# Recurrent layer of a two-layer encoder: scans, gelus and products behind the last convolution, the square root in another form, and the split of two weight slabs on another engine

## The chip, the core and the metric

The kernel runs on one core of a Trainium2 chip. TensorE (PE) multiplies matrices, VectorE (DVE), ScalarE (ACT) and GpSimd (POOL) work elementwise, and SyncE (SP) issues most of the DMA transfers. Each engine works through its own queue of instructions in order and waits on semaphores for the others. The metric is the device time of one execution in microseconds; the median of three runs is 1107.1 us (1106.69 to 1107.58).

## The reference

The input is a sequence of 512 tokens of width 1024. Two layers each add a mixer and a squared-relu MLP to it, with an RMS norm ahead of each. The mixer of the first layer is a stick-breaking attention, that of the second the gated recurrent block which the change is about:

```python
proj = h @ w_in
gate = jax.nn.gelu(proj[..., :RG_WIDTH])
xc = causal_depthwise_conv(proj[..., RG_WIDTH:], conv_w, conv_b)
xh = xc.reshape(B, S, RG_BLOCKS, RG_BLOCK_DIM)
r = jax.nn.sigmoid(jnp.einsum('bshi,hij->bshj', xh, w_a).reshape(B, S, RG_WIDTH) + b_a)
i = jax.nn.sigmoid(jnp.einsum('bshi,hij->bshj', xh, w_x).reshape(B, S, RG_WIDTH) + b_x)
log_a = (-RG_C * r.astype(jnp.float32)) * jax.nn.softplus(-lam.astype(jnp.float32))
a = jnp.exp(log_a)
mult = jnp.sqrt(-jnp.expm1(2.0 * log_a))
bterm = mult * (i * xc).astype(jnp.float32)
_, hs = lax.associative_scan(lru_combine, (a, bterm), axis=1)
y = hs.astype(h.dtype) * gate
return y @ w_o
```

All matrices are float32, and the recurrence runs along the 512 tokens: each state is a times the state before it plus bterm.

## The kernel before

Activations lie transposed: 128 of the 1024 features on the partitions, 512 tokens along the free axis, so a layer's activation is eight chunks (C = 8) of 128 x 512. To keep float32 accuracy with fast matmuls, each operand is split into a rounded part and the rest (`wh`, `wl` for weights, `xgh`, `xgl` or `bh`, `bl` for activations), and a product takes three matmuls (`three`, lines 187 to 191). A weight slab of 128 x 1024 is loaded by SP, rounded on ACT (line 178) and then gets its rest in one of two ways: DVE subtracts (line 184), or, while `adding[0]` is set, POOL negates the rounded part (line 181) and a DMA that adds brings the raw slab to it (line 182). Six buffers for the parts run ahead of the matmuls.

Ahead of the layer, `residual` (line 626) adds each chunk of the MLP's output to the stream (`add_x`, line 624), splits it (`halves`: `xgh` on ACT at line 117, `xgl` on DVE at line 118), squares it on ACT (line 138) and lets POOL sum the squares into `ssq` (line 139). A matmul with ones (line 143) sums over the partitions, and `inv_rms` turns that into `r` (lines 123 and 124).

The recurrent layer runs over chunks by a list written out by hand (line 978 on). Its steps are:

- `conv(c)`: a slab product of 24 matmuls in `dense_in`, times `r` (line 906), the convolution as one scaled copy on ACT (line 914, `begin`) and three taps on DVE (line 916, the last is `tap`), then the split of the result on ACT (line 922) and DVE (line 923), and the gate weights. These steps are issued with high priority.
- `gates(c)`: six matmuls (lines 933 to 935) that read this split, two sigmoids on ACT (lines 938 and 939), and a product on DVE (line 940).
- `recur(chunks)`: for three chunks at a time, tanh and exp on ACT (lines 949 and 951), products on DVE and POOL (lines 952 to 954), then the square root on ACT (line 957), a product (line 958) and the scan on DVE (line 959).
- `gate(c)`: a slab product of 24 matmuls and a product with `r` (line 965).
- `gated(chunks)`: gelu on ACT (line 971), the product with the scan's result on DVE (line 973), and the split into `bh` and `bl` (lines 974 and 975), which the product with w_ro reads.

Sigmoid and tanh, exp, square root and gelu need different activation tables, and each change of table is a load on ACT. `after(x)` holds an instruction back until x has been issued on its engine; beyond that, the order on ACT, DVE, POOL and SP is set when the program is built, by a scheduler that simulates the engines. The order on PE within the layer is the order of the program.

The steps at the end of the list are conv 7, the recurrence of chunks 3 to 5, gates 6, gate 5, gated 0 to 5, gate 6, gates 7, the recurrence of chunks 6 and 7, gate 7, gated 6 and 7. Behind it four columns of w_ro (lines 990 to 997) are multiplied chunk by chunk. The buffer tags that matter are `a0` and `tanh` with two buffers each, `aa` with five, `bt` with six (it holds `xc`), `om` with eight, `z` with six.

Of the kernel before, what the change touches and what calls it, by code (L numbers as in the profile page):

```python
# [11 lines left out]
F32 = mybir.dt.float32  # L12
F32R = mybir.dt.float32r
AF = mybir.ActivationFunctionType
ALU = mybir.AluOpType
PSUM = bass.MemoryType.PSUM

P = 128
S = 512
# [28 lines left out]
def hybrid_encoder(  # L48
# [24 lines left out]
    V, A, G, PE = nc.vector, nc.scalar, nc.gpsimd, nc.tensor  # L73
# [15 lines left out]
    def f(ap):  # L89
        return ap.bitcast(F32)  # L90
# [4 lines left out]
    def col(name):  # L95
        o, n = COLS[name]
        return colt[:, o : o + n]
# [68 lines left out]
    adding = [False]  # L166
# [46 lines left out]
    with ExitStack() as actx:  # L213
# [252 lines left out]
        turns = [0]  # L466
# [366 lines left out]
    with ExitStack() as rctx:  # L833
        rp1 = rctx.enter_context(tc.tile_pool(name="rp1", bufs=1))
        rp2 = rctx.enter_context(tc.tile_pool(name="rp2", bufs=2))
        rctx.enter_context(tc.manual_schedule(engines={mybir.EngineType.PE}))


        lam = col("lam")

        def small(name):
            return rp1.tile([P, C], F32, tag=name, name=name)

        ab, pp, den, s1, s2, pl, c8, c4 = (
            small(n) for n in ("ab", "pp", "den", "s1", "s2", "pl", "c8", "c4")
        )
        V.tensor_scalar(ab, lam, -1.0, None, ALU.mult)
        V.tensor_tensor(ab, ab, lam, ALU.max)
        A.activation(pp, ab, AF.Sigmoid, scale=-1.0)
        V.tensor_scalar(den, pp, -1.0, 2.0, ALU.mult, ALU.add)  # L850
        V.reciprocal(den, den)
        V.tensor_tensor(s1, pp, den, ALU.mult)
        V.tensor_tensor(s2, s1, s1, ALU.mult)
        V.tensor_scalar(pl, s2, 1.0 / 17, 1.0 / 15, ALU.mult, ALU.add)
        for n in (13, 11, 9, 7, 5, 3, 1):
            V.tensor_tensor(pl, pl, s2, ALU.mult)
            V.tensor_scalar(pl, pl, 1.0 / n, None, ALU.add)
        V.tensor_tensor(pl, pl, s1, ALU.mult)
        V.tensor_scalar(den, lam, -1.0, 0.0, ALU.mult, ALU.max)
        V.scalar_tensor_tensor(c8, pl, 2.0, den, ALU.mult, ALU.add)  # L860
        V.tensor_scalar(c4, c8, RG_C * 0.5, None, ALU.mult)
        V.tensor_scalar(c8, c8, -RG_C, None, ALU.mult)


        graws = []
        for i in range(2):
            t = rp1.tile([P, 2, P], F32, tag=f"graw{i}", name=f"graw{i}")
            G.memset(t, 0.0)
            graws.append(t)

        def gate_weights(c):
            raw = graws[c % 2]
            for j in range(2):
                a = slice(j * HD, (j + 1) * HD)
                nc.sync.dma_start(out=raw[a, :, a], in_=w_gate[a, c])
            wh = rp2.tile([P, 2, P], F32R, tag="gh", name="gh", bufs=3)
            wl = rp2.tile([P, 2, P], F32R, tag="gl", name="gl", bufs=3)
            A.copy(wh, raw)
            V.tensor_tensor(wl, raw, f(wh), ALU.subtract)
            return wh, wl  # L880

        cw = col("conv")
        r = None
        mark = None

        def after(act):

            return tc.issue_after(act.ins) if act is not None else nullcontext()

        xc, aa, om, z, hs, gin = {}, {}, {}, {}, {}, {}  # L890
        turns = [0, 0]

        def dense_in(i):

            nonlocal r
            adding[0] = turns[0] >= 4
            ps = dense(w_in[i], xgh, xgl, tag=("acc", "t")[turns[0] % 2])
            turns[0] += 1
            if r is None:
                r = sq.inv_rms()  # L900
            return ps

        def conv(c):

            ps = dense_in(C + c)
            V.tensor_tensor(ps, ps, r, ALU.mult)
            aa[c], xc[c], om[c] = (
                rp1.tile([P, S], F32, tag=t, name=t, bufs=n)
                for t, n in (("aa", 5), ("bt", 6), ("om", C))
            )  # L910
            x0 = xc[c]
            nonlocal begin, tap
            taps = [cw[:, i * C + c : i * C + c + 1] for i in range(4)]
            begin = A.activation(x0, ps, AF.Identity, bias=col("conv_b")[:, c : c + 1], scale=taps[3])
            for d in range(1, 4):
                tap = V.scalar_tensor_tensor(
                    x0[:, d:], ps[:, : S - d], taps[3 - d], x0[:, d:], ALU.mult, ALU.add
                )

            i = C - 3 + c % 3  # L920
            xch, xcl = bh[:, i, :], bl[:, i, :]
            A.copy(xch, x0)
            V.tensor_tensor(xcl, x0, f(xch), ALU.subtract)
            gin[c] = (xch, xcl, *gate_weights(c))

        def gates(c):
            nonlocal sig
            xch, xcl, gh, gl = gin[c]
            pg = []
            for i in range(2):  # L930
                pi = bank("oozz"[turns[1] % 4])
                turns[1] += 1
                PE.matmul(pi, gh[:, i, :], xch, start=True, stop=False)
                PE.matmul(pi, gl[:, i, :], xch, start=False, stop=False)
                PE.matmul(pi, gh[:, i, :], xcl, start=False, stop=True)
                pg.append(pi)
            with after(mark):
                A.activation(aa[c], pg[0], AF.Sigmoid, bias=col("b_a")[:, c : c + 1])
                sig = A.activation(om[c], pg[1], AF.Sigmoid, bias=col("b_x")[:, c : c + 1])
            V.tensor_tensor(xc[c], om[c], xc[c], ALU.mult)  # L940

        def recur(chunks):
            nonlocal mark

            for c in chunks:
                a0 = rp2.tile([P, S], F32, tag="a0", name="a0")
                th = rp2.tile([P, S], F32, tag="tanh", name="tanh")
                with after(sig):
                    ex = A.activation(th, aa[c], AF.Tanh, scale=c4[:, c : c + 1])
                with after(ex):  # L950
                    ex = A.activation(a0, aa[c], AF.Exp, scale=c8[:, c : c + 1])
                V.scalar_tensor_tensor(a0, a0, 1.0, th, ALU.add, ALU.mult)
                G.tensor_scalar(aa[c], a0, -1.0, 1.0, ALU.mult, ALU.add)
                V.scalar_tensor_tensor(om[c], a0, 2.0, a0, ALU.subtract, ALU.mult)
            for c in chunks:
                with after(ex):
                    mark = A.activation(om[c], om[c], AF.Sqrt, scale=-1.0)
                V.tensor_tensor(xc[c], xc[c], om[c], ALU.mult)
                V.tensor_tensor_scan(om[c], aa[c], xc[c], 0.0, ALU.mult, ALU.add)
                hs[c] = om[c]  # L960

        def gate(c):
            ps = dense_in(c)
            z[c] = rp1.tile([P, S], F32, tag="z", name="z", bufs=6)
            V.tensor_tensor(z[c], ps, r, ALU.mult)

        def gated(chunks):
            for c in chunks:

                with after(mark), after(begin):  # L970
                    A.activation(z[c], z[c], AF.Gelu_apprx_tanh)
                with after(tap):
                    V.tensor_tensor(z[c], hs[c], z[c], ALU.mult)
                A.copy(bh[:, c, :], z[c])
                V.tensor_tensor(bl[:, c, :], z[c], f(bh[:, c, :]), ALU.subtract)

        sig = begin = tap = None
        for what, c in (
            (conv, 0), (conv, 1), (conv, 2), (gate, 0), (gates, 0), (gates, 1), (conv, 3), (gates, 2),
            (gate, 1), (conv, 4), (gates, 3), (recur, range(3)), (gate, 2), (conv, 5), (gates, 4),  # L980
            (gate, 3), (conv, 6), (gates, 5), (gate, 4), (conv, 7), (recur, range(3, 6)), (gates, 6),
            (gate, 5), (gated, range(6)), (gate, 6), (gates, 7), (recur, range(6, C)), (gate, 7),
            (gated, range(6, C)),
        ):
            with tc.high_priority() if what is conv else nullcontext():
                what(c)

        adding[0] = False

        begun = {}  # L990
        for c in range(4):
            wh, wl = slab(w_ro[c])
            begun[c] = bank("oozz"[c]), wh, wl
        for k in range(C):
            for c in range(4):
                ps, wh, wl = begun[c]
                three(ps, bh[:, k, :], bl[:, k, :], wh[:, k, :], wl[:, k, :], k == 0, k == C - 1)
# [149 lines left out]
```

## Time and profile before

The profiled execution took 1106.54 us. TensorE is the engine with the most work; a table by stage from the view of windows:

| Stretch (us) | length | PE busy | DVE busy | ACT busy | POOL busy | granted PE clock |
|---|---|---|---|---|---|---|
| 500 to 590 | 90 | 90.00 | 63.29 | 39.11 | 20.92 | 1.00 |
| 590 to 610 | 20 | 18.93 | 6.27 | 6.89 | 8.97 | 1.00 |
| 610 to 630 | 20 | 17.76 | 12.49 | 8.84 | 13.27 | 0.91 |
| 630 to 670 | 40 | 40.00 | 24.10 | 25.94 | 24.10 | 1.00 |
| 670 to 690 | 20 | 20.00 | 17.14 | 15.49 | 9.27 | 1.00 |
| 690 to 710 | 20 | 16.91 | 19.96 | 18.40 | 0.00 | 0.92 |
| 710 to 750 | 40 | 40.00 | 28.03 | 20.23 | 7.85 | 1.00 |
| 750 to 850 | 100 | 100.00 | 65.33 | 49.56 | 5.44 | 1.00 |
| whole span | 1104.80 | 1079.34 | 769.53 | 564.49 | 221.25 | 0.993 |

The recurrent layer lies between about 598 and 732 us. A stretch in which PE's busy time falls short of the length is one in which it waited, and the granted clock below 1.00 says that the array ran at reduced speed for a part of it. A row of a timeline gives the start, the duration, the engine, the line, the operation with the tile that it writes and those that it reads, and in brackets the idle time before it with what ended that.

### The profile page before, as it was taken

How to read it: one execution, taken by the hardware profiler on the slowest of the kernel's cores; microseconds unless marked ns; L12 is line 12 of the kernel's file. 1: busy time of each engine (PE TensorE's matmuls, PEld its weight loads, DVE VectorE, ACT ScalarE, POOL GpSimd, SP SyncE). 2: the span in 40 equal slices, each digit the busy share in tenths (PEclk: the TensorE clock that was granted, in tenths of full speed). 3: DMA queues.
4: the chain of work that ended last, by engine and by line, in shares of the span. 5: the costliest groups of instructions: out<-in, count | busy, mean ns of one | idle time of the engine just before them, and what ended most of it. 6: DMA issues, size and time to landing. Idle time of an engine off the chain costs nothing.

```text
span 1104.8 us, 13615 instructions
## 1 busy us (share of the span) xinstructions
PE 1079.3 (98%) x5052; PEld 893.6 (81%) x5052; DVE 769.5 (70%) x984; ACT 564.5 (51%) x831; POOL 221.2 (20%) x232
## 2 busy tenths in 40 slices
PE   9999999998999999999999899899999999999997
PEld 7888888786888888888888688788888888888886
DVE  7878787729694597599465558956695597599522
ACT  6766676726446444344344467844446344343422
POOL 2444444523000000001223655022000000002220
PEclk9999999999999999999999999999999999999999
DMA  7735453426205305302333775242305305303502
GB/s 236 201 100 138 129 140 94 156 71 228 96 1 189 116 1 190 115 1 77 114 109 114 165 166 153 76 154 94 96 20 174 112 20 174 112 1 93 174 1 77
DMA packets 43458, 123.62 MB, mean 112 GB/s; under 512 B 7680, under 2 KB 8448, under 8 KB 43392
## 3 DMA queue, kind: packets, MB, share of 16 engines
q1 hardware_dynamic: 41088, 115.94, 33.3%
q0 software_dynamic: 1728, 6.29, 3.0%
q8 instruction: 40, 0.66, 0.2%
q10 hardware_dynamic: 576, 0.52, 0.1%
q14 instruction: 26, 0.21, 0.1%
HBM read 101.76 MB, written 2.10 MB: 94 GB/s over the span
## 4 chain that ended last, share of the span: by engine, by line
PE 90%; DVE 4%; ACT 3%; DMA 1%; issue 1%; POOL 0%; SPq 0%; DVEq 0%; ACTq 0%; POOLq 0%
PE ps_acc L190 7%; PE ps_acc L189 7%; PE ps_acc L191 7%; PE ps_o L191 4%; PE ps_o L189 4%; PE ps_o L190 4%; PE ps_t L190 4%; PE ps_t L189 4%; PE ps_t L191 4%; PE ps_z L189 3%; PE ps_z L190 3%; PE ps_z L191 3%; PE ps_t L758 2%; PE ps_t L757 2%; PE ps_t L759 2%; PE ps_acc L758 2%
## 5 line engine op out<-in xcount | busy, mean ns | idle before, releaser
L178 ACT CAST wh<-raw 128x1024 fp32r<-128x1024 f32 (+2 forms) x144 | 128.6, 911 | 159.1 <-PE ps_o L191 47.2
L184 DVE TENSOR_TENSOR wl<-raw,wh 128x1024 fp32r<-128x1024 f32 (+2 forms) x132 | 143.9, 1103 | 30.1 <-ACT wh L178 30.0
L690 POOL TENSOR_TENSOR bl<-u,bh 128x512 fp32r<-128x512 f32 x16 | 31.4, 1962 | 556.5 <-ACT bh L689 540.8
L189 PE MATMUL ps_acc<-xgh,wh 128*128 128x512 f32 x320 | 128.2, 401 | 1.3 <-ACT xgh L117 1.1
L732 ACT CAST wh<-b 128x1024 fp32r<-128x1024 f32 x72 | 75.7, 1051 | 102.5 <-PE ps_acc L759 16.2
L191 PE MATMUL ps_acc<-xgl,wh 128*128 128x512 f32 x320 | 126.0, 394 | 0.3 <-DVE xgl L118 0.3
L190 PE MATMUL ps_acc<-xgh,wl 128*128 128x512 f32 x320 | 126.1, 394 | 0.0
L733 DVE TENSOR_TENSOR wl<-b,wh 128x1024 fp32r<-128x1024 f32 x72 | 88.0, 1222 | 27.0 <-ACT wh L732 27.0
L493 DVE TENSOR_TENSOR_SCAN scan<-keep,later 128x128 f32<-128x128 f32 (+1 forms) x64 | 56.8, 888 | 22.3 <-ACT keep L485 15.9
L191 PEld LDWEIGHTS ps_acc<-xgl,wh 128*128 128x128 f32 x320 | 60.5, 189 | 13.9 <-DVE xgl L118 0.8
L189 PEld LDWEIGHTS ps_acc<-xgh,wh 128*128 128x128 f32 x320 | 60.6, 189 | 12.6 <-ACT xgh L117 1.5
L190 PEld LDWEIGHTS ps_acc<-xgh,wl 128*128 128x128 f32 x320 | 60.6, 189 | 10.8 <-DVE wl L160 0.5
L685 ACT ACTIVATE u<-u 128x512 f32<-128x512 f32 x64 | 39.6, 630 | 54.4 <-DVE u L684 54.3
L189 PE MATMUL ps_t<-xgh,wh 128*128 128x512 f32 x168 | 67.0, 399 | 0.0
L190 PE MATMUL ps_t<-xgh,wl 128*128 128x512 f32 x168 | 66.6, 397 | 0.0
L191 PE MATMUL ps_t<-xgl,wh 128*128 128x512 f32 x168 | 66.3, 395 | 0.0
L191 PE MATMUL ps_o<-xgl,wh 128*128 128x512 f32 x152 | 60.4, 397 | 3.9 <-DVE xgl L118 3.9
L497 POOL TENSOR_TENSOR w<-w,scan 128x128 f32<-128x128 f32 (+1 forms) x64 | 52.5, 822 | 56.9 <-DVE scan L493 55.6
L189 PE MATMUL ps_o<-xgh,wh 128*128 128x512 f32 x152 | 61.3, 403 | 0.0
L190 PE MATMUL ps_o<-xgh,wl 128*128 128x512 f32 x152 | 59.8, 394 | 0.0
L189 PE MATMUL ps_z<-xgh,wh 128*128 128x512 f32 x128 | 50.0, 391 | 0.0
L190 PE MATMUL ps_z<-xgh,wl 128*128 128x512 f32 x128 | 49.9, 389 | 0.0
(339 smaller groups left out, 2791.1 us busy)
## 6 DMA issues: line engine op xcount, KB each, us to landing
raw<-in_w_m SPq DMA_DIRECT2D x72, 512.0 KB, 3.5
b<-in_w_dn SPq DMA_DIRECT2D x36, 512.0 KB, 4.3
raw<-in_w_in SPq DMA_DIRECT2D x16, 512.0 KB, 3.5
raw<-in_w_qk SPq DMA_DIRECT2D x12, 512.0 KB, 3.8
raw<-in_w_dn SPq DMA_DIRECT2D x12, 512.0 KB, 3.5
wl<-raw POOLq DMA_DIRECT2D x12, 512.0 KB, 5.1
x<-in_xT SPq DMA_DIRECT2D x16, 256.0 KB, 3.9
raw<-in_w_ro SPq DMA_DIRECT2D x8, 512.0 KB, 3.4
```

The costliest lines, as they stand in the source:

```text
L178: A.copy(wh[:, k, :], raw[:, k, :])
L184: V.tensor_tensor(wl[:, k, :], raw[:, k, :], f(wh[:, k, :]), ALU.subtract)
L189: PE.matmul(ps, wh, ah, start=start, stop=False)
L190: PE.matmul(ps, wl, ah, start=False, stop=False)
L191: PE.matmul(ps, wh, al, start=False, stop=stop)
L493: V.tensor_tensor_scan(sc[:, S - n : S][:, ::-1], keep[:, :n][:, ::-1], later[:, S - n :][:, ::-1], 1.0, ALU.mult, ALU.max,)
L497: G.tensor_tensor(wt, wt, sc[:, S - n + 1 : S + 1], ALU.mult)
L685: A.activation(t, t, AF.Square)
L690: G.tensor_tensor(bl[:, c, :], t, f(bh[:, c, :]), ALU.subtract)
L732: A.copy(wh, raw)
L733: V.tensor_tensor(wl, raw, f(wh), ALU.subtract)
L758: PE.matmul(ps[i], h[:, piece, ts], wl[:, jj, :], start=False, stop=False)
```

## The change

The subtraction on DVE serves two more slabs of w_in: `adding` is set from the seventh slab on and no longer from the fifth. The conv's split gives its two instructions the names `high` and `low`. The sigmoids of `gates` are issued behind the last conv's scaled copy. In `recur`, with t = tanh, 1 - a^2 is written as t (1 + a)^2, so that the root is sqrt(t) (1 + a): tanh is written into `om`, `d` takes the place of the tile `tanh`, (1 + a) is multiplied into `xc`, and the root reads t. The scans of chunks 0 to 5 are issued behind the last tap, the gelus behind `high` and the products behind `low` of the last conv. Some lines move by one or two (952 to 958 keep their numbers; the scan is now 961, gate's product 967, gelu 972, the product 974, the split 975 and 976).

```diff
         def dense_in(i):
 
             nonlocal r
-            adding[0] = turns[0] >= 4
+            adding[0] = turns[0] >= 6
...
             xch, xcl = bh[:, i, :], bl[:, i, :]
-            A.copy(xch, x0)
-            V.tensor_tensor(xcl, x0, f(xch), ALU.subtract)
+            high = A.copy(xch, x0)
+            low = V.tensor_tensor(xcl, x0, f(xch), ALU.subtract)
...
-            with after(mark):
+            with after(mark), after(begin):
                 A.activation(aa[c], pg[0], AF.Sigmoid, bias=col("b_a")[:, c : c + 1])
                 sig = A.activation(om[c], pg[1], AF.Sigmoid, bias=col("b_x")[:, c : c + 1])
...
             for c in chunks:
                 a0 = rp2.tile([P, S], F32, tag="a0", name="a0")
-                th = rp2.tile([P, S], F32, tag="tanh", name="tanh")
+                d = rp2.tile([P, S], F32, tag="d", name="d")
                 with after(sig):
-                    ex = A.activation(th, aa[c], AF.Tanh, scale=c4[:, c : c + 1])
+                    ex = A.activation(om[c], aa[c], AF.Tanh, scale=c4[:, c : c + 1])
                 with after(ex):
                     ex = A.activation(a0, aa[c], AF.Exp, scale=c8[:, c : c + 1])
-                V.scalar_tensor_tensor(a0, a0, 1.0, th, ALU.add, ALU.mult)
-                G.tensor_scalar(aa[c], a0, -1.0, 1.0, ALU.mult, ALU.add)
-                V.scalar_tensor_tensor(om[c], a0, 2.0, a0, ALU.subtract, ALU.mult)
+                V.scalar_tensor_tensor(d, a0, 1.0, om[c], ALU.add, ALU.mult)
+                G.tensor_scalar(aa[c], d, -1.0, 1.0, ALU.mult, ALU.add)
+                V.scalar_tensor_tensor(xc[c], a0, 1.0, xc[c], ALU.add, ALU.mult)
             for c in chunks:
                 with after(ex):
-                    mark = A.activation(om[c], om[c], AF.Sqrt, scale=-1.0)
+                    mark = A.activation(om[c], om[c], AF.Sqrt)
                 V.tensor_tensor(xc[c], xc[c], om[c], ALU.mult)
-                V.tensor_tensor_scan(om[c], aa[c], xc[c], 0.0, ALU.mult, ALU.add)
+
+                with after(tap if c < 6 else None):
+                    V.tensor_tensor_scan(om[c], aa[c], xc[c], 0.0, ALU.mult, ALU.add)
                 hs[c] = om[c]
...
         def gated(chunks):
             for c in chunks:
-
-                with after(mark), after(begin):
+                with after(mark), after(high):
                     A.activation(z[c], z[c], AF.Gelu_apprx_tanh)
-                with after(tap):
+                with after(low):
                     V.tensor_tensor(z[c], hs[c], z[c], ALU.mult)
                 A.copy(bh[:, c, :], z[c])
                 V.tensor_tensor(bl[:, c, :], z[c], f(bh[:, c, :]), ALU.subtract)
```

More of the change, by code (lines that the diff above doesn't have):

```diff
@@ L911, in conv @@
             x0 = xc[c]
-            nonlocal begin, tap
+            nonlocal begin, tap, high, low
             taps = [cw[:, i * C + c : i * C + c + 1] for i in range(4)]
@@ L975, in gated @@
                 V.tensor_tensor(bl[:, c, :], z[c], f(bh[:, c, :]), ALU.subtract)
-        sig = begin = tap = None
+        sig = begin = tap = high = low = None
         for what, c in (
```

## The prediction

> **What bounds the kernel now.** I read the page first, then the list of what TensorE waited for, then the timelines of the stretch from 596 to 716 us, where the recurrent layer lies.
>
> ```profile
> span 1104.8 us, 13615 instructions
> PE 1079.3 (98%) x5052; PEld 893.6 (81%) x5052; DVE 769.5 (70%) x984; ACT 564.5 (51%) x831; POOL 221.2 (20%) x232
> PE 90%; DVE 4%; ACT 3%; DMA 1%; issue 1%; POOL 0%; SPq 0%; DVEq 0%; ACTq 0%; POOLq 0%
> ```
>
> TensorE sets the time: 98% busy, 90% of the chain that ended last. The order of its instructions is the same in both built programs, so the change can only take away or add TensorE waits. Between 600 and 760 us these are all of them:
>
> ```profile
> PE ps_z L935 <- DVE bl L923: 3.1, 1, 3.1
> PE ps_z L143 <- POOL ssq L139: 1.9, 1, 1.9
> PE ps_acc L189 <- ACT xgh L117: 1.1, 1, 1.1
> PE ps_acc L191 <- DVE xgl L118: 0.3, 1, 0.3
> ```
>
> Two places, then: the last three rows are the end of the norm before the layer, the first is the gates of chunk 7. A timeline shows what they cost (start, duration, the wait in brackets):
>
> ```profile
> 608.50 0.39 PE L191 MATMUL ps_acc<-xgl,wh 128*128 128x512 f32 x1
> 609.95 0.50 PE L189 MATMUL ps_acc<-xgh,wh 128*128 128x512 f32 x1 [1.06 <-ACT xgh L117]
> 611.01 0.50 PE L191 MATMUL ps_acc<-xgl,wh 128*128 128x512 f32 x1 [0.33 <-DVE xgl L118]
> 613.43 1.13 PE L143 MATMUL ps_z<-ssq,ones 128*128 128x512 f32 x2 [1.92 <-POOL ssq L139]
> ...
> 614.66 0.63 PE L190 MATMUL ps_t<-xgh,wl 128*128 128x512 f32 x1
> ...
> 618.03 0.40 PE L189 MATMUL ps_t<-xgh,wh 128*128 128x512 f32 x1
> ...
> 703.15 0.40 PE L934 MATMUL ps_z<-bh,gl 128*128 128x512 f32 x1
> 706.64 0.75 PE L935 MATMUL ps_z<-bl,gh 128*128 128x512 f32 x1 [3.09 <-DVE bl L923]
> ...
> 710.17 0.40 PE L190 MATMUL ps_t<-xgh,wl 128*128 128x512 f32 x1
> 710.40 0.39 PE L191 MATMUL ps_t<-xgl,wh 128*128 128x512 f32 x1
> ```
>
> At full speed one matmul follows the other after 710.40 - 710.17 = 0.23 us. The wait at L935 lasts from 703.38 (703.15 + 0.23) to 706.64: 3.26 us. Then the array runs slowly: 706.64 to 710.17 is eight steps in 3.53 us instead of 8 x 0.23 = 1.84, so 1.69 us more. The first place has the same tail: 614.66 to 618.03 is eight steps in 3.37 us, 1.53 us more.
>
> **The change, part by part.**
>
> *Two slabs from POOL to DVE.* The fifth and sixth slab of w_in are split by DVE (L184) and no longer by POOL (L181) and an adding transfer (L182).
>
> ```profile
> 608.23 0.69 DVE L624 TENSOR_TENSOR x<-x,ps_t 128x512 f32<-128x512 f32 x1 [2.76 <-PE ps_t L191]
> 609.38 2.77 POOL L181 TENSOR_SCALAR wl<-wh 128x1024 fp32r<-128x1024 f32 x1 [0.45 <-ACT wh L178]
> 609.81 0.62 ACT L138 ACTIVATE sq<-x 128x512 f32<-128x512 f32 x1
> 612.12 1.25 POOL L139 TENSOR_TENSOR ssq<-ssq,sq 128x512 f32<-128x512 f32 x1
> ...
> 759.30 0.69 DVE L624 TENSOR_TENSOR x<-x,ps_acc 128x512 f32<-128x512 f32 x1 [2.46 <-PE ps_acc L191]
> 760.39 1.23 DVE L184 TENSOR_TENSOR wl<-raw,wh 128x1024 fp32r<-128x1024 f32 x1 [0.40 <-ACT wh L178]
> 761.53 0.75 DVE L118 SCALAR_TENSOR_TENSOR xgl<-x,colt,xgh 128x512 fp32r<-128x512 f32 x1
> 761.64 1.78 POOL L139 TENSOR_TENSOR ssq<-ssq,sq 128x512 f32<-128x512 f32 x1 [3.66 <-ACT sq L138]
> ```
>
> The last square is ready at 610.43 (609.81 + 0.62), but POOL is busy with L181 until 612.15, and only then adds it to the sum that L143 reads. The rows at 759 to 762 are the next norm, where DVE already splits the slab in the order that the new program has here: L624, L184, L118, with L139 free to start. Laid on this place (608.23 for 759.30), L184 starts at 609.32, L118 at 610.46 and L139 at 610.57, ending 1.78 later at 612.35. L143 then starts at about 612.4 instead of 613.43: **1.0 us** gained. L118 ends at 611.2, 0.2 later than now, and its matmul with it; that stays in front of the sum and costs nothing. The two more L184 (2 x 1.23 us) lie in DVE's idle time before L624 (2.76 us in the row) and under the wait for the sum. If that cover were gone, each L184 would cost its 1.2 us.
>
> Whether the slow tail of 1.53 us stays is open. These rows show two waits of nearly one length, with different ends:
>
> ```profile
> 103.92 0.44 PE L509 MATMUL ps_t<-ident,w 128*128 128x128 f32 x2 [2.09 <-DVE tl L523]
> 104.43 0.40 PE L190 MATMUL ps_acc<-xgh,wl 128*128 128x512 f32 x1
> ...
> 203.52 0.44 PE L509 MATMUL ps_t<-ident,w 128*128 128x128 f32 x2 [2.17 <-DVE tl L523]
> 204.97 0.63 PE L531 MATMUL ps_o<-tl,v 128*128 128x512 f32 x1
> ```
>
> After 2.09 us the next matmul takes 0.40, after 2.17 us matmuls fall to 0.63, 1.4 us later. The new first place would idle 1.2 + 0.7 + 0.9 = 2.8 us in three pieces within 3.7 us, against 1.2 + 0.5 + 2.1 now: between the two rows in kind, so 0 to 1.53 us saved; near neither end, I take the middle, **0.75 us**. The Trainium skill, TensorE: Matmul & The Clock Gate, "What's actually happening", states that the clock halves after an idle window of about 3.4 us that runs freely, so the phase decides; taken literally no wait under 3.4 us could do it, and the row at 204.97 speaks against that. By it the whole 1.53 us would be saved.
>
> *The square root.* sqrt(t)(1+a) has as many DVE products, POOL products and activations per chunk as before; tanh goes into `om` and the new `d` has the two buffers of the old tile. The table loads come in the same number. What goes is one wait: the root needed L954's result, now it only needs tanh, and that L952 has read it.
>
> ```profile
> 683.88 0.69 DVE L952 SCALAR_TENSOR_TENSOR a<-a,tanh 128x512 f32<-128x512 f32 x1 [1.22 <-ACT a L951]
> 689.75 1.30 DVE L184 TENSOR_TENSOR wl<-raw,wh 128x1024 fp32r<-128x1024 f32 x1 [0.25 <-ACT wh L178]
> 691.07 0.39 PE L935 MATMUL ps_o<-bl,gh 128*128 128x512 f32 x1
> 691.69 0.63 ACT L957 ACTIVATE om<-om 128x512 f32<-128x512 f32 x1 [1.44 <-DVE om L954]
> 692.18 1.21 DVE L959 TENSOR_TENSOR_SCAN om<-aa,bt 128x512 f32<-128x512 f32 x1
> 693.32 0.67 DVE L906 TENSOR_TENSOR ps_acc<-ps_acc,r 128x512 f32<-128x512 f32 x1
> 693.29 1.28 ACT L938 ACT_TABLE_LOAD   x1
> 695.74 0.78 ACT L914 ACTIVATE bt<-ps_acc,colt 128x512 f32<-128x512 f32 x1
> 701.16 3.09 DVE L973 TENSOR_TENSOR z<-om,z 128x512 f32<-128x512 f32 x5
> 704.16 1.22 DVE L184 TENSOR_TENSOR wl<-raw,wh 128x1024 fp32r<-128x1024 f32 x1
> 705.90 0.69 DVE L923 TENSOR_TENSOR bl<-bt,bh 128x512 fp32r<-128x512 f32 x1
> ```
>
> *What stands ahead of L923 of chunk 7.* Now six products L973 and a split stand there: 701.16 to 705.90, 4.7 us, and L935 waits for them. In the new order they come behind it, but the three scans of chunks 3 to 5 come ahead of it. I walk the new DVE order from 683.88 with 0.62 us a step (3.09 / 5), 1.2 for L184, 1.14 for a scan (693.32 - 692.18). To L923 of chunk 6 there are ten steps (three each of the two products, the third tap, a gate product, the first root product, L923): it ends at 690.1. Its reader is the L935 at 691.07, so **1.0 us of slack**; now it ends earlier. Then L184 (691.3), two root products (692.5), L906 of chunk 7 (693.1, now 693.32 + 0.67), L184 and two taps (695.6). The next product needs the sigmoid: on ACT, L914 after L906 (693.9), the table load of 1.28 (695.1), two sigmoids of 0.6 (696.35). So product 697.0, tap 697.6, three scans 701.0, L923 701.7. L935 could go at 703.38: **1.7 us of slack**, the wait of **3.26 us** is gone, and the slow tail of **1.69 us** with it.
>
> What is late next: the gelus start after the last conv's copy, 698.2 on ACT, load 699.5, five gelus 702.1; products behind L923 and a gate product from 702.3 to 705.4, L184, the sixth product, and the first subtract (new line 976) writes `bl` at 707.7. TensorE runs gate 7 in 704.3 to 709.9 (24 x 0.23) and reads it from there on: 2.2 us of slack, and 12 x 0.23 = 2.8 us a chunk after that against 0.62. The sigmoids of chunk 7 free the last two banks at 709.3 and 709.9 on ACT; they are needed at 711.3 and 712.0. One w_ro cast now stands in front of chunk 7's tanh and waits for gate 7's end; chunk 6 then reaches `bl` at 722.8, needed at 727. Loads on SP wait for splits that move by 1 us and feed matmuls 20 us off. All later work is paced by TensorE, so the gain reaches the end.
>
> **Sum:** 1.0 + 0.75 + 3.26 + 1.69 = 6.7 us. The profiled execution took 1106.54 us (span 1104.8 and 1.7 around it), so 1099.84; the median of the three runs, 1107.1, is 0.56 above it: **1100.4 us**.
>
> **The rivals.**
> 1. *The clock stays up at the norm*, since no single gap left there is over 1.2 us: the row at 103.92 speaks for it, the one at 204.97 against. It saves 1.53 - 0.75 = 0.8 us more: 1099.6. The Trainium skill's page named above, taken literally, says the same.
> 2. *The DVE walk is 1 to 3 us late.* For it: the 1.0 us of slack at chunk 6, and steps that stretch beside other work (L184 took 1.30 us at 689.75 and 1.22 at 704.16). Against: at 683.88 DVE was waiting, so it starts on time. A wait of up to 2 us comes back at either L935, with or without the tail of 1.69: 1101.4 to 1104.
> 3. *The scans only take the products' place* and the 3.26 us and the tail stay: for it, 3.4 us of scans against 4.7 of products and split; against, these scans no longer stand ahead of L906 and the taps, which start earlier. Then only the norm is gained: 1107.1 - 1.75 = 1105.4.
> 4. *Slower:* the chain L914, table load, sigmoid, product, tap, scans into L923 of chunk 7 has no other work to hide behind on DVE. Each us past 703.4 costs TensorE 1 us, and the tail returns. It breaks even where L923 ends 1.75 us later than now (706.59), at 708.3, 6.6 us past the walk. At 8 us past, 1108.5. For it, only that ACT and DVE hand over three times in it; nothing in the rows is that late.
>
> **How the numbers follow.** Forecast 0.52, rival 1 0.22, rival 2 0.15, rival 3 0.06, rival 4 0.05. The forecast's own ends are 1099.6 and 1101.2 by the clock's bounds. The range is 1099.0 to 1103.2: at the low end the repeat spread of the runs (0.4 us) below rival 1, at the high end most of rival 2. Measurements tell 0.2% (2.2 us) from no change, so faster begins below 1104.9: forecast, rivals 1 and 2, 0.89; same: rival 3 and the milder half of 4, 0.08; slower 0.03.
>
> **What would show it.** The list of TensorE's waits should have no L935 row, or one under 1 us; L143's wait under 1 us; L139 of the last chunk with no L181 ahead of it; scans between the last taps and L923 of chunk 7, that ending near 1.6 us before TensorE wants it; L923 of chunk 6 about 1 us before its reader. After the norm, steps of 0.43 or of 0.23 decide between the forecast and rival 1. I am wrong if a new row of over 2 us stands in the list, or if the steps behind gate 7 are still slow.

## The result, and the profile after

The changed kernel takes 1099.38 us in the median of four runs (1098.16 to 1100.48), beside 1107.14 us for the kernel before: a ratio of 0.993, with a 95% interval of 0.9912 to 0.9947. The forecast was 1100.4 us in a range of 1099.0 to 1103.2. The profiled execution took 1099.0 us, with a span of 1097.3 instead of 1104.8 us. On the page of the kernel after, the span, the busy time of the engines and the chain that ended last read:

```profile
span 1097.3 us, 13621 instructions
PE 1075.0 (98%) x5052; PEld 890.0 (81%) x5052; DVE 772.1 (70%) x986; ACT 563.4 (51%) x831; POOL 216.7 (20%) x228
PE 91%; DVE 4%; DMA 2%; ACT 1%; issue 1%; SPq 1%; POOL 0%; DVEq 0%; ACTq 0%; POOLq 0%
```

PE has the same 5052 matmuls. Its busy time is 4.3 us less (1075.0 for 1079.3) with no matmul left out, so a part of the gain is matmuls that run faster, not waits that are gone. The list of what PE waited for between 590 and 760 us (line, releaser, us in total, times, longest):

```profile
PE ps_acc L189 <- ACT xgh L117: 1.1, 1, 1.1
PE ps_z L143 <- POOL ssq L139: 0.6, 1, 0.6
PE ps_acc L191 <- DVE xgl L118: 0.6, 1, 0.6
```

The row of L935 is gone, and the wait for the sum of squares went from 1.9 to 0.6 us. The view of windows for the two stretches in which the kernel before had a granted clock of 0.91 and 0.92 (window, its length, busy time of PE, PEld, DVE, ACT and POOL, clock, DMA share, GB/s) has the clock at 1.00 in both:

```profile
610.00:630.00 20.00, 18.80 (x78) 14.55 (x79) 14.56 (x17) 9.34 (x12) 12.91 (x7) 1.00 0.44 108
690.00:710.00 20.00, 20.00 (x89) 16.33 (x88) 18.91 (x26) 18.00 (x25) 0.26 (x1) 1.00 0.23 80
```

Where the time went can be read off PE's timeline after, at the same instructions as before:

```profile
611.27 0.50 PE L191 MATMUL ps_acc<-xgl,wh 128*128 128x512 f32 x1 [0.57 <-DVE xgl L118]
612.41 1.12 PE L143 MATMUL ps_z<-ssq,ones 128*128 128x512 f32 x2 [0.63 <-POOL ssq L139]
612.97 0.79 PE L189 MATMUL ps_t<-xgh,wh 128*128 128x512 f32 x1
613.60 0.39 PE L190 MATMUL ps_t<-xgh,wl 128*128 128x512 f32 x1
...
688.45 0.39 PE L935 MATMUL ps_o<-bl,gh 128*128 128x512 f32 x1
...
700.54 0.40 PE L934 MATMUL ps_z<-bh,gl 128*128 128x512 f32 x1
700.77 0.39 PE L935 MATMUL ps_z<-bl,gh 128*128 128x512 f32 x1
...
707.30 0.40 PE L189 MATMUL ps_o<-bh,wh 128*128 128x512 f32 x1
```

L143 starts at 612.41, 1.02 us earlier than before (613.43). Behind it the matmuls follow at full speed, where the kernel before had eight slow steps: 1.53 us. L935 of chunk 7 follows L934 after 0.23 us without a wait: 3.26 us. And no slow stretch comes behind it: 1.69 us. Together 1.02 + 1.53 + 3.26 + 1.69 = 7.50 us, and the spans differ by 7.5. Elsewhere the two executions differ too (one slow stretch begins near 205 us before, and near 106 us after), but up to the last add of the MLP's output this cancels: it starts at 608.23 before and 608.25 after.

The timelines of DVE, POOL and ACT after show why the two waits are gone:

```profile
608.25 0.69 DVE L624 TENSOR_TENSOR x<-x,ps_t 128x512 f32<-128x512 f32 x1 [2.51 <-PE ps_t L191]
609.33 1.23 DVE L184 TENSOR_TENSOR wl<-raw,wh 128x1024 fp32r<-128x1024 f32 x1 [0.39 <-ACT wh L178]
610.47 0.75 DVE L118 SCALAR_TENSOR_TENSOR xgl<-x,colt,xgh 128x512 fp32r<-128x512 f32 x1
610.58 1.77 POOL L139 TENSOR_TENSOR ssq<-ssq,sq 128x512 f32<-128x512 f32 x1 [3.69 <-DVE wl L184]
...
686.76 0.68 DVE L923 TENSOR_TENSOR bl<-bt,bh 128x512 fp32r<-128x512 f32 x1
687.01 1.15 ACT L957 ACTIVATE om<-om 128x512 f32<-128x512 f32 x2
...
693.81 0.69 DVE L940 TENSOR_TENSOR bt<-om,bt 128x512 f32<-128x512 f32 x1 [0.85 <-ACT om L939]
694.42 0.74 DVE L916 SCALAR_TENSOR_TENSOR bt<-ps_acc,colt,bt 128x509 f32<-128x509 f32 x1
695.08 3.44 DVE L961 TENSOR_TENSOR_SCAN om<-aa,bt 128x512 f32<-128x512 f32 x3
698.44 0.67 DVE L923 TENSOR_TENSOR bl<-bt,bh 128x512 fp32r<-128x512 f32 x1
...
699.63 3.09 DVE L974 TENSOR_TENSOR z<-om,z 128x512 f32<-128x512 f32 x5
...
704.37 3.09 DVE L976 TENSOR_TENSOR bl<-z,bh 128x512 fp32r<-128x512 f32 x5
```

The last add into `ssq` (L139) starts 0.1 us behind L118's start, with no slab in POOL's queue ahead of it. L923 of chunk 6 ends at 686.76 + 0.68 = 687.44, and its reader starts at 688.45: 1.0 us of slack. The three scans stand between the last tap and L923 of chunk 7, which ends at 699.11, 1.66 us ahead of L935 at 700.77. The products that held it up before come behind it, from 699.63 on.

### The profile page after: what moved, and what is told of

It reads as the page before. It is cut to its first block, busy times and chain, and to the rows that moved or that the text cites. A ratio compares the mean times of both kernels' runs of the same rounds, so it can differ in the third digit from the quotient of the medians.

```text
span 1097.3 us, 13621 instructions
## 1 busy us (share of the span) xinstructions
PE 1075.0 (98%) x5052; PEld 890.0 (81%) x5052; DVE 772.1 (70%) x986; ACT 563.4 (51%) x831; POOL 216.7 (20%) x228
## 4 chain that ended last, share of the span: by engine, by line
PE 91%; DVE 4%; DMA 2%; ACT 1%; issue 1%; SPq 1%; POOL 0%; DVEq 0%; ACTq 0%; POOLq 0%
PE ps_acc L189 7%; PE ps_acc L190 7%; PE ps_acc L191 7%; PE ps_o L191 4%; PE ps_t L190 4%; PE ps_t L189 4%; PE ps_t L191 4%; PE ps_o L189 4%; PE ps_o L190 4%; PE ps_z L190 3%; PE ps_z L189 3%; PE ps_z L191 3%; PE ps_t L758 2%; PE ps_t L757 2%; PE ps_t L759 2%; PE ps_acc L758 2%
## 5 line engine op out<-in xcount | busy, mean ns | idle before, releaser
L690 POOL TENSOR_TENSOR bl<-u,bh 128x512 fp32r<-128x512 f32 x16 | 28.2, 1761 | 559.4 <-ACT bh L689 541.5
L189 PE MATMUL ps_acc<-xgh,wh 128*128 128x512 f32 x320 | 128.3, 401 | 1.3 <-ACT xgh L117 1.1
L190 PE MATMUL ps_acc<-xgh,wl 128*128 128x512 f32 x320 | 126.0, 394 | 0.2 <-DVE wl L160 0.2
L189 PEld LDWEIGHTS ps_acc<-xgh,wh 128*128 128x128 f32 x320 | 60.5, 189 | 12.8 <-ACT xgh L117 1.8
L190 PEld LDWEIGHTS ps_acc<-xgh,wl 128*128 128x128 f32 x320 | 60.5, 189 | 10.8 <-DVE wl L160 0.8
L189 PE MATMUL ps_t<-xgh,wh 128*128 128x512 f32 x168 | 66.1, 394 | 0.0
L497 POOL TENSOR_TENSOR w<-w,scan 128x128 f32<-128x128 f32 (+1 forms) x64 | 54.9, 858 | 56.4 <-DVE scan L493 55.0
L190 PE MATMUL ps_t<-xgh,wl 128*128 128x512 f32 x168 | 65.7, 391 | 0.0
L189 PE MATMUL ps_o<-xgh,wh 128*128 128x512 f32 x152 | 61.1, 402 | 0.0
L190 PE MATMUL ps_o<-xgh,wl 128*128 128x512 f32 x152 | 59.7, 393 | 0.0
L189 PE MATMUL ps_z<-xgh,wh 128*128 128x512 f32 x128 | 50.0, 391 | 0.0
L190 PE MATMUL ps_z<-xgh,wl 128*128 128x512 f32 x128 | 49.9, 390 | 0.0
```

The costliest lines, as they stand in the source:

```text
L189: PE.matmul(ps, wh, ah, start=start, stop=False)
L190: PE.matmul(ps, wl, ah, start=False, stop=False)
L497: G.tensor_tensor(wt, wt, sc[:, S - n + 1 : S + 1], ALU.mult)
L690: G.tensor_tensor(bl[:, c, :], t, f(bh[:, c, :]), ALU.subtract)
```

## The experiments

Eight kernels ran, four beside one set of runs of the kernel before (median 1107.72 us) and four beside another (1107.03 us). The first four take the change apart. In the first, the change is whole but for the slabs: POOL splits the fifth and the sixth again.

```diff
-            adding[0] = turns[0] >= 6
+            adding[0] = turns[0] >= 4
```

> The changed kernel, with the adding transfers from the fifth slab on again (as before). Theory (two places add up): the norm's last sum stands behind POOL's negation of a slab again, so TensorE's wait for it is about 1.9 us instead of 0.6, the matmul with ones starts at about 613.4 us instead of 612.4, and the slow steps behind it (1.5 us) come back in most executions; no wait at the gates of chunk 7. Time 1100.4 to 1102.0, about 1.0 to 2.5 us above the changed kernel's 1099.4. Rival (the reordering of the layer is the whole gain): 1099.4, the wait for the sum no matter.

Measured: 1101.03 us, ratio 0.9947 (0.9929 to 0.9965). The waits of the norm are back at 1.1, 0.3 and 1.9 us, and L935 doesn't wait. The second kernel is its counterpart: the kernel before with the slabs alone.

```diff
-            adding[0] = turns[0] >= 4
+            adding[0] = turns[0] >= 6
```

> The kernel before, with DVE splitting two more slabs as in the change and nothing else of it. Theory: the wait for the norm's sum falls from 1.9 to about 0.6 us, the wait of 3.1 us at the gates of chunk 7 stays with its slow steps; time 1104.6 to 1106.1, so 1.0 to 2.5 us below the kernel before. Rival (the slabs bring nothing alone, since the layer behind waits for the same result anyway and takes it up in the wait at chunk 7): 1107.1, with that wait grown to about 4.1 us.

Measured: 1105.09 us, ratio 0.9977 (0.9964 to 0.999). The list of PE's waits has the short wait for the sum, and the old one at L935:

```profile
PE ps_z L935 <- DVE bl L923: 3.1, 1, 3.1
...
PE ps_z L143 <- POOL ssq L139: 0.6, 1, 0.6
```

So the slabs shorten the norm's wait and leave L935 alone, and the rest of the change does the reverse. But PE's timeline of the kernel with the slabs alone shows that the short waits can still be followed by slow matmuls:

```profile
611.46 2.08 PE L143 MATMUL ps_z<-ssq,ones 128*128 128x512 f32 x2 [0.63 <-POOL ssq L139]
612.55 1.42 PE L189 MATMUL ps_t<-xgh,wh 128*128 128x512 f32 x1
613.76 0.63 PE L190 MATMUL ps_t<-xgh,wl 128*128 128x512 f32 x1
...
614.94 0.39 PE L190 MATMUL ps_t<-xgh,wl 128*128 128x512 f32 x1
```

Here L143 and L189 are slow already (2.08 and 1.42 us, where the changed kernel shows 1.12 and 0.79). From L143's start to the second L190 it takes 614.94 - 611.46 = 3.48 us; the changed kernel needs 1.89 for these instructions (612.41 to 614.30). The slow stretch costs 1.59 us, as much as before.

The third kernel is the kernel before with the gelus behind `high` and the products behind `low`, and nothing else. The fourth adds the slabs to it; the old root and the old place of the scans stay in both.

```diff
-            A.copy(xch, x0)
-            V.tensor_tensor(xcl, x0, f(xch), ALU.subtract)
+            high = A.copy(xch, x0)
+            low = V.tensor_tensor(xcl, x0, f(xch), ALU.subtract)
...
-                with after(mark), after(begin):
+                with after(mark), after(high):
                     A.activation(z[c], z[c], AF.Gelu_apprx_tanh)
-                with after(tap):
+                with after(low):
                     V.tensor_tensor(z[c], hs[c], z[c], ALU.mult)
```

> The kernel before, with only the order of gelus and gating products changed (gelus behind the copy, products behind the subtraction of the last convolution); old root, scans where they were, slabs as before. Theory (the products ahead of the subtraction were the wait): the subtraction for chunk 7 ends at about 703.0 us, its reader wants it at 703.4, so the wait falls from 3.1 us to under 0.5 and the slow steps go: 1102.2, up to 1103.2 if the later gelus make TensorE wait for the last two banks. Rival (the new root and the later scans are needed for it): a wait of 1 us or more stays at chunk 7 and the time is 1104 or above.

> The kernel before, with the new order of gelus and products and with the two slabs on DVE; old root, scans where they were. Theory: the gains of the two places add, 1107.1 - 5.0 - 1.0 to 2.5 = 1099.6 to 1101.1, so within 1.5 us of the whole change; what remains between the two is a short wait for the last two banks. Rival (root and scans carry a part of the gain of their own): 1102 or above.

Measured: 1102.67 us, ratio 0.9956 (0.9942 to 0.9969), and with the slabs 1098.39 us, ratio 0.9929 (0.9909 to 0.9949). Neither waits at L935. So the two lines that hold gelus and products back take the whole wait away, and with the slabs they give what the change gives (0.9929 beside 0.993): within the two intervals, some 2 us to each side, neither the new root nor the place of the scans and sigmoids shows time of its own. The expectation of the fourth was 1.2 us too high at its lower end, and the short wait that it names for the last two banks did not come. DVE's and PE's timelines of the fourth show what root, scans and sigmoids do bring:

```profile
701.56 0.69 DVE L923 TENSOR_TENSOR bl<-bt,bh 128x512 fp32r<-128x512 f32 x1
```

```profile
702.67 0.39 PE L935 MATMUL ps_z<-bl,gh 128*128 128x512 f32 x1
```

L923 ends at 702.25, 0.42 us ahead of its reader; in the changed kernel it is 1.66. Together they are worth 1.24 us of slack, which nothing in the changed kernel uses.

The next three test the queue in front of L923. In the fifth, the change is whole but the gelus and products are held as before.

```diff
-                with after(mark), after(high):
+                with after(mark), after(begin):
...
-                with after(low):
+                with after(tap):
```

> The changed kernel, with the gelus and the gating products tied as before (behind the last tap, not behind the subtraction); new root, later scans and the two slabs stay. Theory (what stands ahead of the subtraction of chunk 7 on DVE decides): five products of 0.62 us stand there again, behind the three scans; the subtraction ends at about 702.2 us instead of 699.1, its reader wants it at 700.8, so the wait at chunk 7 is back with 1.0 to 2.2 us, and the slow steps in a part of the executions: 1100.5 to 1103, against 1099.4. Rival (earlier scans' place and root carry the gain): no wait, 1099.4.

Measured: 1102.88 us, ratio 0.9957 (0.9939 to 0.9975). Its DVE timeline has the scans and then the products and a gate product ahead of L923; PE's shows what that costs:

```profile
698.49 2.47 DVE L974 TENSOR_TENSOR z<-om,z 128x512 f32<-128x512 f32 x4
700.88 0.68 DVE L967 TENSOR_TENSOR z<-ps_t,r 128x512 f32<-128x512 f32 x1
701.48 0.68 DVE L974 TENSOR_TENSOR z<-om,z 128x512 f32<-128x512 f32 x1
702.08 0.68 DVE L923 TENSOR_TENSOR bl<-bt,bh 128x512 fp32r<-128x512 f32 x1
```

```profile
702.81 0.50 PE L935 MATMUL ps_z<-bl,gh 128*128 128x512 f32 x1 [1.84 <-DVE bl L923]
703.15 0.40 PE L933 MATMUL ps_z<-bh,gh 128*128 128x512 f32 x1
```

The wait of 1.84 us is the one expected, and in this execution the matmuls behind it follow at full speed. PE loses 2.00 us here (from 700.81, when L935 could have gone, to 702.81), where the second experiment, with the old root and the old place of the scans, loses 3.25 (701.41 to 704.66). So where the two lines are missing, the 1.24 us of root, scans and sigmoids do shorten the wait. The eight runs lie in two groups: four from 1098.96 to 1101.16 us with a mean granted clock of 0.997 to 0.998, and four from 1104.6 to 1106.17 us with 0.991 to 0.993. The median lies between them, and the one profile, of a run in the first group, doesn't show what the second group lost.

The sixth and the seventh kernel keep the change and put two and six more products, each of the size of one L974, into DVE's queue ahead of L923 of chunk 7. Their results are not used.

```diff
+            pad = tap
+            if c == C - 1:
+                spare = work.tile([P, S], F32, tag="sq", name="spare")
+                for _ in range(2):
+                    with after(pad):
+                        pad = V.tensor_tensor(spare, r, r, ALU.mult)
...
-            low = V.tensor_tensor(xcl, x0, f(xch), ALU.subtract)
+            with after(pad):
+                low = V.tensor_tensor(xcl, x0, f(xch), ALU.subtract)
```

> The changed kernel with two more products of 128x512 on DVE ahead of the subtraction of chunk 7 (1.2 us). Theory (1.66 us of slack there): the subtraction ends at about 700.3, its reader starts at 700.8, no wait at chunk 7, time as the changed kernel's, 1099.4 (1098 to 1100.5). Rival (the slack is not real, since TensorE is let go by something later): a wait of about 1.2 us and 1100.6.

> The same with six more products ahead of the subtraction of chunk 7; a gate product and a split move ahead of it as well, together 6 x 0.62 + 0.6 + 1.2 = 5.5 us. Theory: 5.5 - 1.66 of slack = a wait of 3.5 to 3.9 us at chunk 7 and slow steps of 1.0 to 1.7 us behind it: 1103.8 to 1105.0, that is 4.4 to 5.6 above the changed kernel. Rival (a wait there is taken up later, by work behind it that waits for something else anyway): under 2 us above it.

Measured: 1099.54 us with two, ratio 0.9935 (0.992 to 0.995), and 1105.7 us with six, ratio 0.999 (0.998 to 0.9999). With two, DVE's and PE's timelines (the lines are seven further down, L942 is the old L935) read:

```profile
699.59 0.69 DVE L930 TENSOR_TENSOR bl<-bt,bh 128x512 fp32r<-128x512 f32 x1
```

```profile
700.74 0.39 PE L942 MATMUL ps_z<-bl,gh 128*128 128x512 f32 x1
```

L923 ends at 700.28 instead of 699.11, and 0.46 us of the slack is left: 1.66 less two products of 0.6 each. Time that lies within the slack is free. With six the slack is used up, and PE waits at the old place again:

```profile
700.50 0.40 PE L941 MATMUL ps_z<-bh,gl 128*128 128x512 f32 x1
704.72 0.79 PE L942 MATMUL ps_z<-bl,gh 128*128 128x512 f32 x1 [3.82 <-DVE bl L930]
...
710.26 0.39 PE L189 MATMUL ps_t<-xgh,wh 128*128 128x512 f32 x1
```

The wait costs 704.72 - 700.73 = 3.99 us, and the 13 steps from 704.72 to 710.26 take 5.54 us instead of 13 x 0.23 = 2.99: 2.55 us more. Together that is 6.5 us, and the kernel is 6.3 us slower than the changed one. The expectation was 0.7 us too low at its upper end because it took at most 1.7 us for the slow stretch.

The eighth kernel tries to gain more at the norm: the changed kernel, with the casts of the slabs five to seven on ACT issued behind the norm's square root, so that neither they nor the splits that need them stand among the last chunk's work.

```diff
+            behind[0] = root[0] if 4 <= turns[0] <= 6 else None
...
-            A.copy(wh[:, k, :], raw[:, k, :])
+            with tc.issue_after(behind[0].ins) if behind[0] is not None else nullcontext():
+                A.copy(wh[:, k, :], raw[:, k, :])
```

> The changed kernel, with the splits of the fifth to seventh slab issued on ACT behind the norm's square root, so that no cast stands between the last sum and its split. Theory: what is left of the waits at the norm (1.1 + 0.6 + 0.6 us) is the cast of 1.05 us and the split of 1.2 us ahead of the split of the last chunk; the matmul with ones then starts 0.5 to 0.9 us earlier, at 611.5 to 611.9 us, the first wait falls to about 0.7, and the time to 1098.5 to 1098.9. Rival (the later casts delay the first convolutions and TensorE waits for those): a new wait between 615 and 650 us and 1099.4 or above.

Measured: 1099.84 us, ratio 0.9938 (0.9926 to 0.9951). Its DVE and PE timelines around the norm's end (L628, L145 and L194 are the old L624, L143 and L190):

```profile
610.01 0.69 DVE L628 TENSOR_TENSOR x<-x,ps_t 128x512 f32<-128x512 f32 x1 [3.25 <-PE ps_t L195]
```

```profile
613.44 1.44 PE L145 MATMUL ps_z<-ssq,ones 128*128 128x512 f32 x2 [0.64 <-POOL ssq L141]
...
615.10 0.63 PE L194 MATMUL ps_t<-xgh,wl 128*128 128x512 f32 x1
...
617.61 0.39 PE L194 MATMUL ps_t<-xgh,wl 128*128 128x512 f32 x1
```

From the last add to the sum's matmul it is 3.43 us instead of 4.16 (608.25 to 612.41): 0.73 us gained, as expected. But a slow stretch follows: 4.17 us from L145 to the third L194 behind it (617.61), where the changed kernel takes 2.58 (612.41 to 614.99), 1.59 us more. The median missed the 1098.5 to 1098.9 us that were expected, and in the total time the kernel can't be told from the change. The new wait that the rival names didn't come: PE's list up to 760 us has the 0.84 and 0.64 us at the norm and nothing else.

## Why the prediction came out

*The slabs, 1.0 us: right.* L143 is 1.02 us earlier, the order on DVE and POOL is the one of the next norm, and L118's matmul is 0.26 us later and hidden, as said. The two kernels with one part each confirm that only this edit moves the norm.

*The slow stretch behind the norm, 0.75 us: the term that was mis-sized.* The prediction took the middle between 0 and 1.53 us. In the profiled execution the whole 1.53 us went, which is rival 1, and the measured 1099.38 us lies nearer to that rival's 1099.6 than to the forecast's 1100.4. It is also where the sum fell short: the profiled executions are 7.5 us apart, 0.8 more than the 6.7 forecast, and 1.53 - 0.75 is 0.8. The runs show that there is no middle: the stretch comes whole or not at all, since the clock is halved for a whole window of 3.41 us (shown in the last section). It cost 1.56 us in the kernel before, 1.56 in the first experiment, 1.59 in the second, 1.61 in the third and 1.59 in the eighth, each from L143's start against the changed kernel's own steps. What the slabs change is how often. With the long wait it came in all three profiled executions (before, first, third), with the short waits in two of seven (second and eighth, but not in the changed kernel and the fourth to seventh). By these few executions the term is 1.6 x 5/7 = 1.1 us in the mean. Rival 1's reason doesn't hold either: the second and eighth experiment have no single gap over 1.1 us at the norm, and the clock fell. That it stayed up in the profiled execution of the changed kernel was luck of the windows.

*The root: right, and not needed.* The root no longer waits for DVE (the row at 687.01 has no bracket), and chunk 6 has the 1.0 us of slack that was worked out. The third and fourth experiment do without it and show no loss.

*L923 of chunk 7, 3.26 + 1.69 us: right.* On the axis of the kernel before, which the gain at the norm shifts by 1.02 + 1.53 = 2.55 us, the walk's end of L923 at 701.7 is 699.15; it ended at 699.11. The walk's product at 697.0 is 694.45, and it ended at 694.50; the first `bl` at 707.7 is 705.15, and the row of L976 starts at 704.37 with 0.62 for each, so 705.0, 2.3 us before the product with w_ro begins at 707.30. The fifth experiment shows that it is the products in DVE's queue that made the wait, the sixth that the slack is real, and the seventh that the wait and the slow stretch come back together once it is used up. That answers rival 3, too: scans in the products' place are harmless, since they alone fit into the slack.

*Rivals 2 and 4* didn't occur: no step of the walk into L923 was over 0.2 us late. The step that would decide rival 4, a wait on DVE for the sigmoid of chunk 6 (L940 at 693.81), is there, but 0.85 us long.

*The size of the second slow stretch* was right for this change, but 1.69 us isn't its general price: behind a wait of 3.8 us it cost 2.55 us in the seventh experiment, and behind one of 3.1 us, as long as in the kernel before, 2.73 in the second (13 steps from 704.66 to 710.38). In both the clock was halved for two windows instead of one (last section).

## What to carry to other kernels

On an engine that works in order, a product that nobody waits for delays the split that TensorE waits for, if it stands ahead of it: two lines that held the gelus and products behind the split took away the whole wait, while the rewritten root and the moved scans only added slack. Count a wait of TensorE, or several short ones close together, with the slow matmuls that can come behind it (here nothing, or 1.5 to 2.7 us), so removing 3.3 us can bring 5. And where a term hangs on the clock, take it as a chance with a full price rather than as a middle value.

## What the runs showed of the hardware

**The slow stretch comes in whole windows.** The view of windows shows how long the granted clock is down (columns as in the section on the result). The first two rows are of the kernel before, the next two of the second experiment, the last two of the changed kernel:

```profile
703.31:706.72 3.41, 0.32 (x3) 0.08 (x1) 3.41 (x6) 3.39 (x7) 0.00 (x0) 1.00 0.12 23
706.72:710.13 3.41, 3.41 (x8) 2.69 (x9) 3.41 (x6) 3.31 (x5) 0.00 (x0) 0.50 0.33 131
...
607.97:611.38 3.41, 1.23 (x3) 0.48 (x3) 1.91 (x3) 2.04 (x4) 1.74 (x1) 1.00 0.21 54
703.54:710.37 6.83, 5.71 (x13) 4.46 (x14) 6.83 (x11) 6.65 (x9) 0.00 (x0) 0.50 0.27 92
...
607.13:610.54 3.41, 2.34 (x10) 1.42 (x8) 1.90 (x3) 2.19 (x3) 0.00 (x0) 1.00 0.17 70
610.54:613.95 3.41, 2.21 (x7) 1.17 (x7) 0.68 (x2) 2.12 (x2) 2.77 (x2) 1.00 0.40 154
```

In all ten traces the clock is at 1.00 or 0.50, and each stretch at 0.50 before the end of the program lasts 3.41 us or, three times, 6.83. Within an execution their starts lie whole multiples of 3.41 us apart: in the kernel before they are 204.96, 266.40, 614.56 and 706.72, so 18, 102 and 27 windows. Half the clock over one window of work loses 3.41 / 2 = 1.7 us, near the 1.5 to 1.7 measured; in the second and seventh experiment there were two windows, the first of which began while PE still waited. The clock's fall goes with how little PE worked within one such window: of the windows at full clock up to there, all 22 with less than 1.5 us of PE's busy time were followed by one at 0.50, two of 16 with 1.5 to 1.95 us, and none with more. So the same waits at the norm cost 1.6 us or nothing, by where the windows lie: the second experiment has only 1.23 us of work in one of them, the changed kernel 2.34 and 2.21 in two. This is read off the traces; no run moved the windows alone.

**A wait need not be 3.4 us long.** The changed kernel's own PE timeline has the case that the prediction's two rows left open, the other way round: a wait of 2.08 us ends at 104.33, and matmuls are slow from 105.67 on.

```profile
104.33 0.44 PE L509 MATMUL ps_t<-ident,w 128*128 128x128 f32 x2 [2.08 <-DVE tl L523]
...
105.67 0.63 PE L189 MATMUL ps_acc<-xgh,wh 128*128 128x512 f32 x1
```

In the kernel before, 2.09 us at the same instruction left the clock up, and 2.17 us near 204 us brought it down. At the norm, waits of 0.6 to 1.1 us, three in the second experiment and two (0.84 and 0.64) in the eighth, were enough. The Trainium skill, TensorE: Matmul & The Clock Gate, "What's actually happening", names an idle window of about 3.4 us, which runs freely, as what halves the clock. The traces agree on the length and on windows that keep one rhythm through an execution; but windows in which PE was busy for 0.32 to 1.92 us brought the clock down as well, so the measurement decides against that rule taken literally.

**The spread goes with the clock.** The 41 runs of the kernel before beside the experiments lie between 1103.08 and 1110.03 us, and they are the longer the lower the mean granted clock: 1103.08 us in the one run at 0.998, a median of 1106.78 in the 20 at 0.993, and of 1109.1 in the nine at 0.990. That is some 0.75 us for each 0.001, so a difference of 1 us between two kernels, such as that between the changed kernel and the fourth experiment, can be a difference of clocks.

**A one-input operation on POOL can stretch.** In POOL's timeline of the changed kernel the last of three equal instructions (L953 at 685.72) took 4.54 us and the one before it 1.00. It isn't chance: in the other five traces with the new root the same instruction took 4.54 or 4.55 us too, and in the four with the old one 1.02. It did no harm, since the scan that reads it is the third of the three from 695.08 on and the operation ended at 690.26. Spans on POOL are rough, and its cause was not tried.
